# First projection cut into quarters of x and of its weights, with idle products ahead of them and the parameter rows moved ahead of the second megabyte of weights

## The chip, the cores and the metric

One core of a Trainium2 chip runs the whole program. The metric is device time in microseconds (us). The engines are TensorE (PE; its weight loads are shown apart as PEld), VectorE (DVE), ScalarE (ACT), GpSimd (POOL) and SyncE (SP). In this kernel SP issues nearly all DMAs. Each engine works through its own instructions in a fixed order, and an instruction that waits holds up everything behind it on its engine.

## The reference, cut to what matters

One decoder layer on x of 256 tokens by 1024 channels, float32:

```python
def mixer(x, w_in, ...):
    proj = jnp.einsum("bsd,de->bse", x, w_in)          # 1024 -> 10264 columns
    (a_in, gdn_qkv, gdn_beta_in, gdn_decay_in, gdn_gate_in,
     sb_qkv, gla_qkv, gla_lr, gla_gate_in, merge_in) = jnp.split(proj, offsets, axis=-1)
    ...
    qkv = jax.nn.silu(causal_depthwise_conv(gdn_qkv, gdn_conv_w))
    g = -jnp.exp(gdn_a_log) * jax.nn.softplus(gdn_decay_in + gdn_dt_bias)
    ...                                                # four mixers, gates, output projection
x = layer_norm(DN_ALPHA * x + mixer(x, ...), ln1_g, ln1_b)
x = layer_norm(DN_ALPHA * x + moe(x, ...), ln2_g, ln2_b)   # 16 experts, top 2
```

The change concerns the first 256 of those 10264 columns (the first part of `gdn_qkv`) and the loads ahead of the second 256.

## The kernel before

The kernel streams `w_in` in pieces of 256 columns, 1 MB each. A piece goes through three raw buffers (`fetch`, line 109). `parts` (line 119) splits each half of it into a high part `whi` (ACT, rounded to the type fp32r) and the remainder `wlo` (DVE). x is split the same way into `xh` and `xl`. `proj_cm` (line 282) then makes, for each half of 128 columns, 16 products with `whi` (lines 271 and 275) and 8 with `wlo` (line 280), 48 a piece, each of 256 columns on PE.

The steps of the mixers stand in a list written by hand, `ORDER` (line 40); it begins `bi.0 cc bi.1 bi.2 cq.0 bi.3 sm`. `bi.0`, `bi.1`, `bi.2` are the first three pieces (here w0, w1, w2), `cc` makes small constants (`aexp` among them, line 353, out of the row `gdn_a_log`). A scheduler puts the instructions of PE, ACT, DVE and POOL into an order of its own by what it thinks will be ready; SP keeps the order of the program.

At the start SP issues x in four pieces of 256 KB (line 145), w0 in two halves of 128 columns, w1 in one piece (line 146), then eleven rows of parameters into the tile `prm_r` (line 165) and two rows, `gdn_a_log` and `gdn_dt_bias`, into `hp8` (lines 177 and 178), then w2 and the rest. A SP DMA uses one of eight completion counters in turn, and its issue waits until the DMA eight places ahead of it has landed. PE transposes x in four groups (line 263), and ACT and DVE split them. `taps` (line 335) transposes `prm_r` on PE (`pp`) and makes the convolution weights `cwh` out of it, which the evictions of w0's products need.

Of the kernel before, what the change touches and what calls it, by code (L numbers as in the profile page):

```python
# [8 lines left out]
F32 = mybir.dt.float32  # L9
# [9 lines left out]
S = 256  # L19
# [32 lines left out]
def trunk(ctx: ExitStack, tc: tile.TileContext, a, out):  # L52
# [55 lines left out]

    def fetch(src, cuts=1):
        k, n = src.shape[1], src.shape[2]  # L110
        turn_raw()
        raw = rwp[rwo[-1]].tile([128, 2048], F32, name="raw", tag="raw")[:, :k * n]
        raw = raw.rearrange("p (k c) -> p k c", k=k)
        for c in range(cuts):
            cs = slice(c * n // cuts, (c + 1) * n // cuts)
            Q.dma_start(raw[:, :, cs], src[:, :, cs])
        return raw

    def parts(raw, k0, nk, c0, n, one=None):

# [4 lines left out]
        src = raw[:, k0:k0 + nk, c0:c0 + n]  # L125
        cuts = (slice(0, nk),) if one is None else (slice(0, nk // 2), slice(nk // 2, nk))
        for c in cuts:
            if one is None:
                A.copy(hi, src)  # L129
            else:  # L130
                A.activation(hi[:, c], src[:, c], AF.Copy, scale=one)  # L131
        for c in cuts:
            V.tensor_tensor(lo[:, c], src[:, c], hi[:, c].bitcast(F32), op=OP.subtract)  # L133
        return hi, lo
# [54 lines left out]
    def late_loads():  # L189
# [67 lines left out]
    xl = xtp.tile([128, 8, S], F32R, name="xl")  # L257
    one0 = cst.tile([128, 1], F32, name="one0")
    for kg in range(2):
        for n in range(2):  # L260
            p = pb("pxt")
            for k in range(4):
                T.transpose(p[:, k, :], x0[n][:, (4 * kg + k) * 128:(4 * kg + k + 1) * 128], ident)
            split(p, xh[:, 4 * kg:4 * kg + 4, n * 128:(n + 1) * 128],
                  xl[:, 4 * kg:4 * kg + 4, n * 128:(n + 1) * 128])
    A.activation(one0, xh[:, 4, 0:1].bitcast(F32), AF.Copy, scale=0.0, bias=1.0)

# [126 lines left out]
    def b_in(ci):  # L394
# [1034 lines left out]
```

## Time and profile before

| | us |
|---|---|
| median of 3 runs | 622.49 (621.53 to 623.31) |
| the profiled execution's own time | 622.35 |
| its span in the trace | 620.6 |
| PE busy | 585.3 (94%) |
| DVE busy | 322.3 (52%) |
| ACT busy | 252.2 (41%) |

The profiled execution stands at the median, and 1.75 us of it lie outside its span. The page's strip of 40 slices of 15.5 us shows where PE is not full: the first slice, a stretch in the middle, and the last ones. Its column of the granted clock reads full in the first slices; there the spacing of the products tells the clock: 256 columns in 0.213 us are 1.2 columns a ns, in 0.118 us near 2.2, so the first belongs to the level of 1.2 GHz and the second to that of 2.4 GHz.

### The profile page before, as it was taken

What the parts mean: (1) busy time and instruction counts of PE and PEld (TensorE: products, weight loads), DVE (VectorE), ACT (ScalarE), POOL (GpSimd) and SP (SyncE); (2) the same over time, 40 slices, a digit from 0 to 9 for tenths busy, and PEclk for the clock granted to TensorE, in tenths of its full rate; (3) what the DMA queues carried; (4) which work ended last, traced back from release to release, by engine and by line L of the source; (5) the groups of instructions that cost most, each with busy time, mean ns of one, the idle gap of its engine ahead of it and who ended that gap; (6) DMA issues with size and microseconds to landing.
All of it is one profiled execution on the core that took longest, in us unless ns stands there. A gap on an engine that the chain in (4) does not pass through costs nothing.

```text
span 620.6 us, 10538 instructions
## 1 busy us (share of the span) xinstructions
PE 585.3 (94%) x4225; PEld 458.0 (74%) x4225; DVE 322.3 (52%) x639; ACT 252.2 (41%) x413; POOL 23.1 (4%) x57
## 2 busy tenths in 40 slices
PE   6999999999988999999999999999999999999970
PEld 5999999999888999999999999533543634533340
DVE  3798888687566976565566655551210210300154
ACT  5557654473569784444444445210211211210121
POOL 3000010000111000000000000000000000000002
PEclk9999999999999999999999998999999999999995
DMA  7877454632221446588999795899999999999912
GB/s 206 240 227 179 137 181 122 215 110 70 69 70 50 155 127 203 197 295 299 376 336 336 272 404 183 295 330 410 419 412 409 417 413 409 418 415 408 418 70 72
DMA packets 86658, 160.93 MB, mean 259 GB/s; under 512 B 9990, under 2 KB 56444, under 8 KB 86604
## 3 DMA queue, kind: packets, MB, share of 16 engines
q1 hardware_dynamic: 86476, 159.94, 71.4%
q8 instruction: 35, 0.57, 0.4%
q0 software_dynamic: 128, 0.26, 0.2%
q14 instruction: 19, 0.16, 0.1%
HBM read 159.01 MB, written 1.18 MB: 258 GB/s over the span
## 4 chain that ended last, share of the span: by engine, by line
PE 70%; issue 12%; DVE 6%; DMA 6%; ACT 3%; POOL 1%; SPq 1%; POOLq 0%; DVEq 0%; ACTq 0%
PE wg L1277 9%; PE pd L1288 9%; PE wu L1277 8%; PE pcm L271 7%; PE pcm L280 7%; PE pcm L275 7%; DMA raw<-in_w_in_dram 3%; PE pxg L1198 3%; PE pbr L271 2%; PE pbr L280 2%; PE pbr L275 2%; DMA ew<-in_w_down_dram 2%; DVE wlo L133 1%; PE pwo L271 1%; PE py L1297 1%
## 5 line engine op out<-in xcount | busy, mean ns | idle before, releaser
L133 DVE TENSOR_TENSOR wlo<-raw,whi 128x1024 fp32r<-128x1024 f32 (+1 forms) x106 | 126.0, 1201 | 53.6 <-ACT whi L129 53.0
L129 ACT CAST whi<-raw 128x1024 fp32r<-128x1024 f32 x102 | 105.9, 1048 | 101.3 <-PE pcm L275 41.7
L271 PE MATMUL pcm<-xh,whi 128*128 128x256 f32 x512 | 126.0, 284 | 2.4 <-ACT whi L131 1.5
L275 PE MATMUL pcm<-xl,whi 128*128 128x256 f32 x512 | 125.0, 282 | 0.0
L271 PEld LDWEIGHTS pcm<-xh,whi 128*128 128x128 f32 x512 | 97.2, 190 | 3.3 <-ACT whi L131 1.9
L275 PEld LDWEIGHTS pcm<-xl,whi 128*128 128x128 f32 x512 | 97.3, 190 | 0.1
L280 PE MATMUL pcm<-xh,wlo 128*128 128x256 f32 x512 | 72.2, 282 | 0.2
L280 PEld LDWEIGHTS pcm<-xh,wlo 128*128 128x128 f32 x512 | 65.5, 189 | 0.7 <-DVE wlo L133 0.6
L101 DVE TENSOR_TENSOR dd<-pd,dd 128x512 fp32r<-128x512 f32 (+1 forms) x18 | 11.4, 631 | 95.2 <-ACT dd L100 95.2
L1288 PE MATMUL pd<-ew,sh 128*64 128x512 f32 (+1 forms) x288 | 57.7, 546 | 2.1 <-DMA ew<-in_w_down_dram 1.3
L1277 PE MATMUL wu<-ew,xg 128*64 128x512 f32 x256 | 57.4, 593 | 0.0
L1277 PE MATMUL wg<-ew,xg 128*64 128x512 f32 x256 | 56.7, 595 | 0.6 <-issue 0.6
L1288 PEld LDWEIGHTS pd<-ew,sh 128*64 128x64 f32 x288 | 20.5, 137 | 37.2 <-issue 29.4
L1277 PEld LDWEIGHTS wu<-ew,xg 128*64 128x64 f32 x256 | 18.5, 137 | 36.2 <-issue 34.4
L1277 PEld LDWEIGHTS wg<-ew,xg 128*64 128x64 f32 x256 | 18.1, 137 | 33.5 <-issue 31.8
L271 PE MATMUL ptm<-whi,xh 128*128 128x256 f32 x128 | 32.6, 287 | 0.0
L271 PE MATMUL pbr<-yth,whi 128*128 128x256 f32 x128 | 32.1, 284 | 0.0
L275 PE MATMUL pbr<-ytl,whi 128*128 128x256 f32 x128 | 32.1, 282 | 0.0
L273 PE MATMUL ptm<-whi,xl 128*128 128x256 f32 x128 | 31.6, 281 | 0.0
L100 ACT CAST dd<-pd 128x512 fp32r<-128x512 f32 (+1 forms) x18 | 9.7, 539 | 48.5 <-PE pd L1288 48.5
L1205 ACT ACTIVATE xg<-pxg,gbp 128x128 f32<-128x128 f32 x32 | 13.3, 456 | 36.8 <-DVE xg L1204 35.8
L1318 DVE SCALAR_TENSOR_TENSOR sh<-wu,cw,sh 128x512 f32<-128x512 f32 x8 | 6.0, 750 | 40.2 <-PE wu L1277 40.1
(410 smaller groups left out, 884.9 us busy)
## 6 DMA issues: line engine op xcount, KB each, us to landing
raw<-in_w_in_dram SPq DMA_DIRECT2D x39, 1024.0 KB, 5.3
ew<-in_w_gate_dram SPq DMA_DIRECT2D x64, 512.0 KB, 10.0
ew<-in_w_up_dram SPq DMA_DIRECT2D x64, 512.0 KB, 9.9
ew<-in_w_down_dram SPq DMA_DIRECT2D x64, 512.0 KB, 9.9
raw<-in_w_branch_dram SPq DMA_DIRECT2D x8, 1024.0 KB
raw<-in_w_out_dram SPq DMA_DIRECT2D x4, 1024.0 KB
x<-in_x_dram SPq DMA_DIRECT2D x4, 256.0 KB, 5.1
raw<-in_w_in_dram SPq DMA_DIRECT2D x2, 512.0 KB
```

What stands on the lines that cost most here:

```text
L100: A.copy(hi, ps)
L101: V.tensor_tensor(lo, ps, hi.bitcast(F32), op=OP.subtract)
L129: A.copy(hi, src)
L133: V.tensor_tensor(lo[:, c], src[:, c], hi[:, c].bitcast(F32), op=OP.subtract)
L271: T.matmul(o, sh(k), mh(k), start=first and k == 0, stop=False)
L273: T.matmul(o, sl(k), mh(k), start=False, stop=False)
L275: T.matmul(o, sh(k), ml(k), start=False, stop=False)
L280: T.matmul(o, sl(k), mh(k), start=False, stop=last and k == kt - 1)
L1198: P(T.matmul(ps[kg][:, k, :], x[:, n, 128 * (2 * kg + k):128 * (2 * kg + k) + 128], oh[n], start=first and n == 0, stop=last and n == 1))
L1205: A.activation(xg[1][:, 2 * kg + k, :], ps[kg][:, k, 128:256], AF.Identity, scale=g_, bias=b_)
L1277: P(T.matmul(p[r, :], xg[pr][:, k, r], W[pr, (nm, e, k // 2)][:, k % 2, :], start=k == 0, stop=k == 7))
L1288: P(T.matmul(p[r, :], hT[:, k, r], W[pr, ("wd", e, k)][:, 0, c0:c1], start=k == 0, stop=k == 3))
```

## The change

- x is loaded in eight pieces of 128 KB and w0 in four of 256 KB (256 rows of the weights each), a quarter of x and a quarter of w0 in turn.
- The thirteen rows of parameters (`prm_r`, `hp8`) follow w0; w1 comes behind them, and w2 is fetched with it.
- `first_proj` replaces `proj_cm` for w0: 14 idle products of a tile of zeros on PE, the transposes of the first quarter of x, 8 more idle products, and then, quarter by quarter, the split of the weights, 8 products with the high part, the transposes of the next quarter of x, and 4 products with the low part. They are kept in this order among themselves; other instructions may be placed between them.
- The helpers for a split in halves (`cuts`, `one`) and the constant `one0` go.

```diff
-    for h in range(2):
-        for n in range(2):
-            Q.dma_start(x0[n][:, 512 * h:512 * h + 512], xin[:, n, 512 * h:512 * h + 512])
-    raw0 = [fetch(w_in[:, :, C_GQ + 256 * j:C_GQ + 256 * j + 256], 2 - j) for j in range(2)]
+    w0 = w_in[:, :, C_GQ:C_GQ + 256]
+    raw0 = [fetch(w0, 0)]
+    for q in range(4):
+        cs = slice(256 * q, 256 * q + 256)
+        for n in range(2):
+            Q.dma_start(x0[n][:, cs], xin[:, n, cs])
+        Q.dma_start(raw0[0][:, 2 * q:2 * q + 2], w0[:, 2 * q:2 * q + 2])
...
+    raw0 += [fetch(w_in[:, :, C_GQ + 256 * j:C_GQ + 256 * j + 256]) for j in (1, 2)]
...
+    def warm(n):
+        for _ in range(n):
+            K(T.matmul(idle, wz[:, 0:128], wz, start=True, stop=True))
+    def x_part(q):
+        ps = pb("pxt", (128, 2, S))
+        for n in range(2):
+            for k in range(2):
+                K(T.transpose(ps[:, k, n * 128:(n + 1) * 128], x0[n][:, (2 * q + k) * 128:(2 * q + k + 1) * 128], ident))
+        split(ps, xh[:, 2 * q:2 * q + 2, :], xl[:, 2 * q:2 * q + 2, :], keep=K)
+    def first_proj():
+        p = pmm.tile([128, 2, S], F32, name="pcm", tag="mm")
...
+        warm(14)
+        x_part(0)
+        warm(8)
+        for q in range(4):
...
+            K(A.copy(hi, raw))
+            K(V.tensor_tensor(lo, raw, hi.bitcast(F32), op=OP.subtract))
+            for k in range(2 * q, 2 * q + 2):
+                for b in range(2):
+                    for x in (xh, xl):
+                        K(T.matmul(p[:, b, :], hi[:, k % 2, 128 * b:128 * b + 128], x[:, k, :],
+                                   start=q == 0 and k == 0 and b == 0 and x is xh, stop=False))
+            if q < 3:
+                x_part(q + 1)
+            low(q)
+        return p
...
-        p = proj_cm(C_GQ + 256 * ci, raw0[ci] if ci < 2 else None, one0 if ci == 0 else None)
+        p = first_proj() if ci == 0 else proj_cm(C_GQ + 256 * ci, raw0[ci] if ci < 3 else None)
```

On SP, before: `raw_109` is w0 in two halves and `raw_112` is w1, ahead of the first parameter rows.

```order
L116 DMA raw_109<-in_w_in_dram 128x8x128 x2
L116 DMA raw_112<-in_w_in_dram 128x8x256
L165 DMA prm_r_114<-in_gdn_conv_w_dram 48x128
L165 DMA prm_r_114<-in_gdn_norm_w_dram 1x128
L165 DMA prm_r_114<-in_gla_b_gate_dram 4x128
```

On SP, now: the end of the parameter rows; `raw_143` is w1, `raw_145` w2 and `raw_496` the piece of `cq.0`.

```order
L163 DMA prm_r_118<-in_rg_b_x_dram 4x128
L163 DMA prm_r_118<-in_rg_lambda_dram 4x128
L163 DMA prm_r_118<-in_ln1_g_dram 8x128
L163 DMA prm_r_118<-in_ln1_b_dram 8x128
L175 DMA hp8_132<-in_gdn_a_log_dram 128x4
L176 DMA hp8_132<-in_gdn_dt_bias_dram 128x4
L117 DMA raw_143<-in_w_in_dram 128x8x256
L117 DMA raw_145<-in_w_in_dram 128x8x256
```

All thirteen rows now stand ahead of w1. The row `in_rg_b_x` is the eighth DMA behind the last quarter of w0 (before, it was the eighth behind w1), so its issue waits for the landing of that quarter.

On ACT, before: the four groups of x, the four quarters of the high part of w0, both halves of w1 (`whi_328`, `whi_356`), and then `aexp`, which reads the row `hp8`.

```order
L131 ACTIVATE whi_217<-raw_109,one0_176 128x512 x2
L131 ACTIVATE whi_247<-raw_109,one0_176 128x512 x2
L129 CAST whi_328<-raw_112 128x1024
L129 CAST whi_356<-raw_112 128x1024
L353 ACTIVATE aexp_209<-hp8_128 128x4
L406 ACTIVATE gq_215<-pcm_216,cwh_206 128x256
```

On ACT, now: `pxt_212`, `pxt_239`, `pxt_260` and `pxt_283` are the four quarters of x, `raw_105` is w0 and `raw_143` is w1.

```order
L102 CAST xh_182<-pxt_239 128x512
L295 CAST whi_227<-raw_105 128x512
L392 ACTIVATE aexp_190<-hp8_132 128x4
L102 CAST xh_182<-pxt_260 128x512
L295 CAST whi_271<-raw_105 128x512
L102 CAST xh_182<-pxt_283 128x512
```

`aexp` moved from behind the splits of w0 and w1 to a place between the second and the third quarter of x. The splits of the third and fourth quarter stand behind it.

On PE, before: the last products of w0 (`pcm_216`), the transpose `pp` of the parameter rows, and the first products of w1 (`pcm_327`).

```order
L275 MATMUL pcm_216<-xl_175,whi_247 128x256
L280 MATMUL pcm_216<-xh_174,wlo_248 128x256 x8
L337 MATMUL pp_277<-ident_98,prm_r_114 128x128
L271 MATMUL pcm_327<-xh_174,whi_328 128x256
L275 MATMUL pcm_327<-xl_175,whi_328 128x256
```

On PE, now: `whi_271` and `wlo_272` are the parts of the third and fourth quarter of w0.

```order
L300 MATMUL pcm_197<-xl_183,whi_271 128x256
L272 MATMUL pxt_283<-ident_98,x0_103 128x128 x2
L272 MATMUL pxt_283<-ident_98,x0_104 128x128 x2
L283 MATMUL pcm_197<-xh_182,wlo_272 128x256 x4
L376 MATMUL pp_308<-ident_98,prm_r_118 128x128
L300 MATMUL pcm_197<-xh_182,whi_271 128x256
```

`pp` moved ahead of the products of the last quarter, so these stand behind the landing of all eleven rows in `prm_r`. Behind the step `sm` every engine's order is that of before.

## Rows read from the trace of the kernel before

**Rows 1.** The page's strip of the span in 40 slices of 15.5 us: busy tenths of PE and of the DMA engines.

```profile
PE   6999999999988999999999999999999999999970
...
DMA  7877454632221446588999795899999999999912
```

**Rows 2.** The table of windows; each row gives the stretch, its length, then busy us (and count) of PE, PEld, DVE, ACT, POOL, the granted clock, the DMA share and GB/s.

```profile
0.00:10.00 10.00, 4.17 (x16) 3.00 (x16) 2.89 (x7) 4.38 (x8) 5.08 (x29) 1.00 0.84 239
10.00:15.00 5.00, 4.88 (x23) 4.88 (x24) 2.79 (x5) 3.28 (x6) 0.00 (x0) 1.00 0.50 159
...
20.00:60.00 40.00, 39.70 (x335) 39.24 (x335) 36.15 (x96) 24.63 (x37) 0.00 (x0) 1.00 0.81 231
...
450.00:584.00 134.00, 134.00 (x664) 56.52 (x662) 20.27 (x41) 20.91 (x41) 0.00 (x0) 1.00 1.03 413
```

**Rows 3.** The chain of work that ended last, followed back from 20 us: start us, us, what. L165 are the parameter rows, L177 and L178 the two rows of `hp8`, L116 pieces of `w_in`.

```profile
3.98 9.74 DMA raw<-in_w_in_dram
...
13.74 0.25 SPq L165
...
15.05 0.36 SPq L177
...
15.46 0.43 SPq L178
...
15.93 0.43 SPq L116
```

**Rows 4.** The waits of SP's queue in the first 20 us: us in total, times, longest us.

```profile
SPq L165 <- DMA raw<-in_w_in_dram: 2.9, 2, 2.6
```

**Rows 5.** The timeline of ACT: start us, us, line, operation, count, and in brackets the idle time before it with its releaser.

```profile
4.75 0.59 ACT L100 CAST xh<-pxt 128x512 fp32r<-128x512 f32 x1 [2.67 <-PE pxt L263]
...
10.88 1.34 ACT L131 ACTIVATE whi<-raw,one 128x512 fp32r<-128x512 f32 x2 [0.20 <-DMA raw<-in_w_in_dram]
13.75 2.00 ACT L129 CAST whi<-raw 128x1024 fp32r<-128x1024 f32 x2 [1.53 <-DMA raw<-in_w_in_dram]
17.59 0.20 ACT L353 ACTIVATE aexp<-hp 128x4 f32<-128x4 f32 x1 [1.85 <-DMA hp<-in_gdn_a_log_dram]
...
21.51 1.05 ACT L129 CAST whi<-raw 128x1024 fp32r<-128x1024 f32 x1 [1.83 <-DMA raw<-in_w_in_dram]
```

**Rows 6.** The timeline of PE in the first projection and at the start of the second (17.98), same columns.

```profile
6.62 1.97 PE L263 MATMUL pxt<-ident,x 128*128 128x128 f32 x8 [0.32 <-DMA x<-in_x_dram]
10.12 0.58 PE L271 MATMUL pcm<-xh,whi 128*128 128x256 f32 x1 [1.53 <-ACT whi L131]
10.51 0.41 PE L275 MATMUL pcm<-xl,whi 128*128 128x256 f32 x1
...
13.71 1.58 PE L280 MATMUL pcm<-xh,wlo 128*128 128x256 f32 x8
15.12 0.28 PE L271 MATMUL pcm<-xh,whi 128*128 128x256 f32 x1
...
17.00 1.11 PE L280 MATMUL pcm<-xh,wlo 128*128 128x256 f32 x8
17.95 0.27 PE L337 MATMUL pp<-ident,prm_r 128*128 128x128 f32 x1
17.98 0.36 PE L271 MATMUL pcm<-xh,whi 128*128 128x256 f32 x1
```

**Rows 7.** The timeline of DVE, same columns: the low parts of w1, and the eviction of the parameter rows.

```profile
14.83 2.36 DVE L133 TENSOR_TENSOR wlo<-raw,whi 128x1024 fp32r<-128x1024 f32 x2 [1.88 <-ACT whi L129]
...
18.26 0.29 DVE L338 COPY prm<-pp 128x128 f32<-128x128 f32 x1 [0.26 <-PE pp L337]
```

**Rows 8.** The table of windows again, by 1 us (columns as in group 2; the last two are the DMA share and GB/s).

```profile
1.00:2.00 1.00, 0.00 (x0) 0.00 (x0) 0.00 (x0) 1.00 (x1) 0.95 (x4) 1.00 0.25 29
...
10.00:11.00 1.00, 0.88 (x4) 0.88 (x5) 0.90 (x2) 0.81 (x3) 0.00 (x0) 1.00 1.08 345
...
12.00:13.00 1.00, 1.00 (x6) 1.00 (x6) 0.94 (x2) 0.22 (x1) 0.00 (x0) 1.00 0.36 107
13.00:14.00 1.00, 1.00 (x7) 1.00 (x6) 0.00 (x0) 0.25 (x1) 0.00 (x0) 1.00 0.02 7
...
18.00:19.00 1.00, 1.00 (x10) 1.00 (x9) 0.70 (x5) 0.13 (x1) 0.00 (x0) 1.00 1.01 352
```

**Rows 9.** The same by 1 us around a gap of PE late in the program; the third column from the right is the granted clock.

```profile
380.00:381.00 1.00, 0.87 (x9) 0.77 (x7) 0.45 (x2) 0.58 (x1) 0.00 (x0) 1.00 0.55 193
381.00:382.00 1.00, 0.51 (x3) 0.28 (x3) 0.78 (x4) 0.50 (x2) 0.00 (x0) 1.00 1.00 410
382.00:383.00 1.00, 0.68 (x5) 0.58 (x6) 0.40 (x5) 0.98 (x2) 0.00 (x0) 1.00 1.09 426
...
384.00:385.00 1.00, 1.00 (x7) 1.00 (x6) 0.99 (x8) 1.00 (x2) 0.00 (x0) 0.50 1.03 418
```

**Rows 10.** The chain of work that ended last, near the end: start us, us, what.

```profile
581.01 3.26 PE wu L1277 x15
584.27 10.28 DMA ew<-in_w_down_dram
...
594.59 2.37 PE pd L1288 x18
```

**Rows 11.** The waits of PE from 20 to 60 us: us in total, times, longest us.

```profile
PE pcm L271 <- DVE splq L326: 0.3, 1, 0.3
```

More of the change, by code (lines that the diff above doesn't have):

```diff
@@ L96, in pb, with split @@
         return pbr.tile(list(shape), F32, name=name, tag="pb")
-    def split(ps, hi, lo, scale=None):
+    K = tc.keep_in_program_order
+    def split(ps, hi, lo, scale=None, keep=lambda i: i):
         if scale is None:
-            A.copy(hi, ps)
-            V.tensor_tensor(lo, ps, hi.bitcast(F32), op=OP.subtract)
+            keep(A.copy(hi, ps))
+            keep(V.tensor_tensor(lo, ps, hi.bitcast(F32), op=OP.subtract))
         else:
@@ L107, in trunk, with fetch @@
     w_in = a["w_in"][0].rearrange("(k p) c -> p k c", p=128)
-    def fetch(src, cuts=1):
+    def fetch(src, rows=None):
         k, n = src.shape[1], src.shape[2]
@@ L113, in fetch, with parts @@
         raw = raw.rearrange("p (k c) -> p k c", k=k)
-        for c in range(cuts):
-            cs = slice(c * n // cuts, (c + 1) * n // cuts)
-            Q.dma_start(raw[:, :, cs], src[:, :, cs])
+        if rows is None:
+            Q.dma_start(raw, src)
         return raw
-    def parts(raw, k0, nk, c0, n, one=None):
+    def parts(raw, k0, nk, c0, n):
         hi = wst.tile([128, 1024], F32R, name="whi", tag="whi", bufs=NHI)[:, :nk * n]
@@ L125, in parts @@
         src = raw[:, k0:k0 + nk, c0:c0 + n]
[L126 to L133, printed above, removed]
+        A.copy(hi, src)
+        V.tensor_tensor(lo, src, hi.bitcast(F32), op=OP.subtract)
         return hi, lo
@@ L257, in trunk @@
     xl = xtp.tile([128, 8, S], F32R, name="xl")
-    one0 = cst.tile([128, 1], F32, name="one0")
-    for kg in range(2):
-        for n in range(2):
[L261 to L266, printed above, removed]
+    wz = cst.tile([128, S], BF16, name="wz")
@@ new lines, in trunk, with low @@
+    V.memset(wz, 0.0)
+    idle = pb("idle", (128, S))
+    def warm(n):
[3 more added lines that the diff above has]
+        ps = pb("pxt", (128, 2, S))
+        for n in range(2):
+            for k in range(2):
[3 more added lines that the diff above has]
+        p = pmm.tile([128, 2, S], F32, name="pcm", tag="mm")
+        hl = {}
+        def low(q):
+            for k in range(2 * q, 2 * q + 2):
+                for b in range(2):
+                    K(T.matmul(p[:, b, :], hl[q // 2][1][:, k % 4, 128 * b:128 * b + 128], xh[:, k, :],
+                               start=False, stop=k == 7 and b == 1))
+        warm(14)
+        x_part(0)
+        warm(8)
+        for q in range(4):
+            if q % 2 == 0:
+                hl[q // 2] = [wst.tile([128, 1024], F32R, name=nm, tag=nm, bufs=NHI).rearrange("p (k c) -> p k c", k=4)
+                              for nm in ("whi", "wlo")]
+            raw = raw0[0][:, 2 * q:2 * q + 2]
+            hi, lo = (t[:, 2 * (q % 2):2 * (q % 2) + 2] for t in hl[q // 2])
+            K(A.copy(hi, raw))
+            K(V.tensor_tensor(lo, raw, hi.bitcast(F32), op=OP.subtract))
+            for k in range(2 * q, 2 * q + 2):
+                for b in range(2):
+                    for x in (xh, xl):
[5 more added lines that the diff above has]
+        return p
@@ L280, in mm3, with proj_cm @@
                 T.matmul(o, sl(k), mh(k), start=False, stop=last and k == kt - 1)
-    def proj_cm(c0, raw=None, one=None):
+    def proj_cm(c0, raw=None):
         if raw is None:
@@ L287, in proj_cm @@
         for b in range(2):
-            hi, lo = parts(raw, 0, 8, 128 * b, 128, one)
+            hi, lo = parts(raw, 0, 8, 128 * b, 128)
             mm3(p[:, b, :], lambda k: hi[:, k, :], lambda k: lo[:, k, :],
```

## The prediction

> **What bounds the kernel now.** I read first the strip and the table of windows. PE is busy 4.17 of the first 10 us, 4.88 of the next 5, 39.70 of the 40 behind them and 134.00 of 134 in the long last stage [rows 1, 2]. So PE is the bound nearly everywhere, and what the change can win lies ahead of about 18 us. What happens to PE there is passed on one for one: the later steps hang on each other, the weight stream of the last stage is issued as PE gives buffers back, and the end itself runs from a PE step at 581.01 through a DMA of 10.28 us back to PE [rows 10]. The orders of all engines behind the step `sm` are the same. I therefore price the change by one number, the time at which PE begins w1's products, 17.98 now [rows 6].
>
> Then the first 18 us. PE waits for x and w0 until 10.12. Its products begin at half clock: 15 of them take 13.71 − 10.51 = 3.20 us, 0.213 each; from about 14.8 they take (17.00 − 15.12)/16 = 0.118, the full clock [rows 6]. The whole first projection is 48 products, 5.7 us at full clock, and it fills 10.12 to 17.95. w1 lands at 13.72, and only then does the row `b_x` go out (13.74): SP waited 2.6 us for that landing. Six issues later, at 15.93, goes w2 [rows 3, 4]. The DMA engines are nearly idle meanwhile: 7 GB/s in the microsecond from 13, 352 again in that from 18 [rows 8]. ACT waits 1.85 us for the row `gdn_a_log`, but has split w1 by then, so nobody waits for it [rows 5].
>
> **What the change removes.** x and w0 are used as they land, so most of the first projection, 7.8 us from 10.12, could run beside the loads. The best it can do is set by the last quarter: its landing, 0.67 us for the high part (1.34 for two halves [rows 5]), 12 products of 0.118, some 2.1 us. When that landing comes, T, is not in the trace. From above: the same two megabytes had landed by 10.88, when ACT could start the second half of w0 [rows 5]. From below: 2.1 MB at 345 GB/s [rows 8] are 6.1 us; transfers begin shortly before 2 (29 GB/s in the microsecond from 1), and the last megabyte landed 1.3 us behind the end of its traffic, which stops at about 12.4 (share 0.36 in that microsecond [rows 8]) and is done at 13.72 [rows 3]; that makes 9.4. Nothing lets it come earlier, since the bytes are the same. I take T = 10.2, the middle. By this alone PE would be free for w1 at 12.3 instead of 17.98. Three moves take it back.
>
> **SP.** `b_x` now waits for T, not for w1. Behind it stand three rows, `gdn_a_log`, `gdn_dt_bias`, and then w1. By the rows of now `gdn_a_log` goes out 15.05 − 13.74 = 1.31 us behind `b_x` and the next megabyte 15.93 − 13.74 = 2.19 [rows 3]. So w1 is issued at T + 2.19 = 12.4. A megabyte issued onto idle queues is there after 5.6 us (w2: 15.93 to 21.51, when ACT starts on it [rows 3, 5]), so w1 lands at 18.0 instead of 13.72. Its split (1.05) puts the first product at 19.05 at best. That alone is 1.1 late.
>
> **ACT.** `aexp` stands now ahead of the splits of the third and fourth quarter and needs `gdn_a_log`. From `b_x` to `aexp` it is 17.59 − 13.74 = 3.85 us now [rows 3, 5], so ACT stands until T + 3.85 = 14.05 with x and w0 long landed. Queued behind it are the high parts of both last quarters, and PE and DVE wait for these. Then `aexp` 0.20, the split of the third quarter of x 0.59 [rows 5], of the weights 0.67: PE restarts at 15.5.
>
> The Trainium skill ("DMA: Bandwidth & Descriptors", "Anatomy of one DMA — SWDGE (gpsimd) path") gives a DMA a fixed cost of about 2.0 us, and its "Rules for kernel authors" call transfers under 64 KB mostly overhead, a rule against putting thirteen of them ahead of a megabyte. The row here took 17.59 − 15.05 = 2.54 us; with the page's figure the sum would be 0.5 less, 625.2 where it is 625.7. The measured row decides.
>
> **PE.** The first two quarters need x and w0's first half. x as a whole is in by 6.62 now, when PE's last eight transposes stop waiting [rows 6], which is about as many bytes. With two splits (1.3) and at most 16 slow slots (3.4) they are done by 11.5. From there to 15.5 PE stands for 4 us. The 22 idle products (22 × 0.213 = 4.7 us at most, of which the first 14 run while PE waited for x anyway) so raise a clock that is lost again: at 381 to 383 PE was busy 0.51 and 0.68 of a microsecond, and the clock of 384 to 385 is 0.50 [rows 9]. The Trainium skill ("TensorE: Matmul & The Clock Gate", "The HAM clock gate") says the same, that an array left idle falls back to 1.2 GHz; these rows agree, and without this fall the sum would be the second rival below.
>
> Restart at 15.5: 8 products of 0.213 (17.2), 4 transposes (0.9, 18.1); ACT then splits the fourth quarter, 0.59 + 0.67 and about 0.05 of handing over: 19.4. Beside that run 4 low products and `pp`, whose rows are in by then (the last one is issued at T + 1.0, two and a half more to land, 13.7). Last come 12 products. Now the clock took 4.6 us of running to rise (10.12 to about 14.8 [rows 6]); the same from 15.5 is 20.1. So 3 at 0.213 and 9 at 0.118 end at 21.2. w1's split ran on ACT from 19.4 to 20.5, hidden. **w1's products begin at 21.2, 3.2 later than 17.98.** If the clock is back by 19.4 it is 20.8, if only behind the last product 22.0.
>
> **What follows.** DVE splits w1 later too: 2.36 us that stood at 14.83, when it was free, now stand behind the eviction `prm` [rows 7]. DVE has 36.15 busy of 40 [rows 2], and PE once waited 0.3 for it [rows 11]. With PE 3.2 later DVE gets that time as well, so I charge nothing; if that cover were short, up to 1 us. The first split of x loses one instruction (`one0`), DVE gains one memset: nothing, both while waiting for x.
>
> The sum goes on the profiled execution: 622.35 + 3.2 = 625.55; the median is 0.14 above that execution, so 625.7.
>
> **Rivals.**
> 1. ACT is released early and w1's landing is the gate. For it: ACT's stop needs only one small row, and w1's landing is gate enough by itself. Against: both hang on the same T, and ACT's part is measured. Then PE ends w0 early, idles until 19.05 and restarts at half clock; 4.6 us at that clock cost about 2.0 over full: 3.1 later, 625.6.
> 2. The clock stays at 2.4 GHz through the 4 us (the idle products having raised it). For it: the gaps in the middle of the program are passed over. Against: rows 9. Then 15.5, 0.94 for 8 products, 0.45 for transposes, 1.31 for the split, 1.42 for 12: 19.65, 1.7 later, 624.2.
> 3. Not slower: SP's rows do not wait for landings. Twelve issues of some 0.46 end at 6.3; eleven rows of 0.33 put `gdn_a_log` at 10.0, landed at 12.5, so PE restarts at 14.0 after a shorter gap and, at full clock, ends w0 at 18.1; w1 issued at 10.8 is in by 16.4. That is 0.15 later, 622.6, no change. It decides from the point where `b_x` leaves before T. Against it: the 2.6 us that `b_x` waits now [rows 4].
>
> **How the numbers follow.** Forecast 0.62; rival 1 0.14; rival 2 0.10; rival 3 0.10; 0.04 for a gain whose place I do not see (part of the 5.7 us kept after all). A difference under 0.3% (1.9 us, so 620.6 to 624.4) is about what a measurement here cannot tell from no change. Faster: 0.04. Same: rival 3 and most of rival 2, 0.16. Slower: 0.80. T's bounds move the forecast by −0.8 and +0.7, the clock by −0.4 and +0.8, DVE's cover by up to +1, so 624.5 to 627.6 for rivals 0 and 1; the range goes down to 623.0 to take in rival 2, and leaves out rival 3, the gain and a small tail above.
>
> **What the changed profile would show.** On ACT, `aexp` at about 14 with an idle stretch of some 4 us ahead of it released by the DMA of `hp`, and the third split of x behind it. On SP, `b_x` at about 10.2 and w1 at 12.4. On PE, nothing from about 11.5 to 15.5, products spaced 0.213 there after, and w1's first product at 21 instead of 18. From there every step later by the same amount. I am wrong if `aexp` is done by 11, if w1's first product stands at 18 or earlier, or if a later stage gives the 3 us back.

## The result and the profile after

The changed kernel takes 628.75 us (median of 5, 626.94 to 630.72) against 622.49 for the kernel before beside it: 1.0103 times as long, 95% interval 1.0082 to 1.0124. It is slower, as forecast, but by 6.3 us and not by 3.2, and outside the range of 623.0 to 627.6. The profiled execution is the median one; its span is 626.9 us, 6.3 more than before.

The start came out nearly as worked out. On SP (timeline: start us, us, line, operation; a row can hold several issues), `b_x` goes out at 10.69, so T was 10.7 where 10.2 was taken; `gdn_a_log` follows at 12.01 and w1 at 12.89, where it went out at 3.98 before [rows 3]:

```profile
10.69 0.25 SPq L163 DMA_DIRECT2D prm_r<-in_rg_b_x_dram  x1
...
12.01 0.36 SPq L175 DMA_DIRECT2D hp<-in_gdn_a_log_dram  x1
...
12.89 11.01 SPq L117 DMA_DIRECT2D raw<-in_w_in_dram  x4
```

On ACT (timeline, in brackets the idle time ahead and its releaser), `aexp` stands 5.23 us for the row of `gdn_a_log`, with the third quarter's splits behind it:

```profile
14.54 0.21 ACT L392 ACTIVATE aexp<-hp 128x4 f32<-128x4 f32 x1 [5.23 <-DMA hp<-in_gdn_a_log_dram]
14.65 0.57 ACT L102 CAST xh<-pxt 128x512 fp32r<-128x512 f32 x1
15.11 0.62 ACT L295 CAST whi<-raw 128x512 fp32r<-128x512 f32 x1
18.75 0.59 ACT L102 CAST xh<-pxt 128x512 fp32r<-128x512 f32 x1 [3.02 <-PE pxt L272]
19.23 0.62 ACT L295 CAST whi<-raw 128x512 fp32r<-128x512 f32 x1
```

On PE, the products of the second quarter still ran at 0.12 us each (10.14 to 10.26), the full clock. The third quarter waits 4.21 us for ACT and starts at 0.21 us a product (16.17 to 16.38), the fourth follows at 19.91, and w1's first product stands at 21.52, against 17.98 [rows 6] and the 21.2 of the forecast:

```profile
10.14 0.28 PE L300 MATMUL pcm<-xl,whi 128*128 128x256 f32 x1
10.26 0.28 PE L300 MATMUL pcm<-xh,whi 128*128 128x256 f32 x1
...
15.79 0.58 PE L300 MATMUL pcm<-xh,whi 128*128 128x256 f32 x1 [4.21 <-ACT whi L295]
16.17 0.41 PE L300 MATMUL pcm<-xl,whi 128*128 128x256 f32 x1
16.38 0.41 PE L300 MATMUL pcm<-xh,whi 128*128 128x256 f32 x1
...
19.91 0.39 PE L300 MATMUL pcm<-xh,whi 128*128 128x256 f32 x1 [0.53 <-ACT whi L295]
...
21.52 0.28 PE L310 MATMUL pcm<-xh,whi 128*128 128x256 f32 x1
```

The table of windows (columns as in [rows 2]) shows the granted clock at 0.50 behind that gap, which is the level of 1.2 GHz, rising again from 18 to 19, then PE full to 60, and the last stage:

```profile
16.00:17.00 1.00, 1.00 (x5) 1.00 (x6) 0.54 (x1) 0.00 (x0) 0.00 (x0) 0.50 1.06 372
18.00:19.00 1.00, 1.00 (x8) 1.00 (x6) 0.00 (x0) 0.25 (x1) 0.00 (x0) 0.62 1.09 352
20.00:60.00 40.00, 39.96 (x337) 39.65 (x338) 37.12 (x99) 25.90 (x41) 0.00 (x0) 1.00 0.76 207
450.00:584.00 134.00, 134.00 (x662) 56.45 (x660) 18.89 (x39) 20.37 (x41) 0.00 (x0) 1.00 1.03 409
```

The last row is the one that was not forecast. In the same stretch the kernel before moved 413 GB/s [rows 2], this one 409, both with the DMA engines' share at 1.03. At the end PE's `pd` (the products of the experts' last weights) waits for `w_down` three times, and its last run begins at 599.98, not at 594.59 [rows 10]:

```profile
597.47 0.65 PE L1327 MATMUL pd<-ew,sh 128*64 128x256 f32 x2 [0.62 <-DMA ew<-in_w_down_dram]
598.72 0.65 PE L1327 MATMUL pd<-ew,sh 128*64 128x256 f32 x2 [0.60 <-DMA ew<-in_w_down_dram]
599.98 2.37 PE L1327 MATMUL pd<-ew,sh 128*64 128x256 f32 x18 [0.62 <-DMA ew<-in_w_down_dram]
```

Places that stand in both kernels in the same order, read from the timelines, show where the 6.3 us arise. `pwt` and `prg` belong to the mixers; `wg`, `wu` and `pd` are the products with the experts' three weights:

| start of | before | after | later by |
|---|---|---|---|
| w1's first product | 17.98 | 21.52 | 3.54 |
| `psmall`, first product of `sm` | 41.16 | 44.13 | 2.97 |
| `pwt`, first transpose | 185.15 | 189.00 | 3.85 |
| `prg`, first product | 211.58 | 216.89 | 5.31 |
| `wg`, first product of the last stage | 394.01 | 397.69 | 3.68 |
| `wu`, last product | 587.28 | 591.16 | 3.88 |
| `pd`, last product | 601.68 | 607.07 | 5.39 |
| the span's end | 620.6 | 626.9 | 6.3 |

So some 3 us come at the start, 1.5 between the last `wu` and the last `pd`, 0.9 behind it. The steps between (+0.9 up to `pwt`, +1.5 near 212, −1.6 ahead of 394) stand in runs without the change too, or fall out either way (below).

### The profile page after: what moved, and what is told of

It is laid out like the page before. It is cut to its first block, busy times and chain, and to the rows that moved or that the text cites. A ratio compares the mean times of both kernels' runs of the same rounds, so it can differ in the third digit from the quotient of the medians.

```text
span 626.9 us, 10585 instructions
## 1 busy us (share of the span) xinstructions
PE 587.6 (94%) x4247; PEld 458.2 (73%) x4247; DVE 321.6 (51%) x640; ACT 251.7 (40%) x412; POOL 23.0 (4%) x57
## 4 chain that ended last, share of the span: by engine, by line
PE 70%; issue 12%; DVE 6%; DMA 6%; ACT 3%; POOL 1%; SPq 0%; POOLq 0%; DVEq 0%; ACTq 0%
PE wg L1316 9%; PE wu L1316 9%; PE pd L1327 9%; PE pcm L310 7%; PE pcm L319 7%; PE pcm L314 7%; PE pxg L1237 2%; DMA raw<-in_w_in_dram 2%; PE pbr L310 2%; PE pbr L319 2%; PE pbr L314 2%; DMA ew<-in_w_down_dram 2%; DVE wlo L128 1%; PE pwo L310 1%; PE py L1336 1%
## 5 line engine op out<-in xcount | busy, mean ns | idle before, releaser
L128 DVE TENSOR_TENSOR wlo<-raw,whi 128x1024 fp32r<-128x1024 f32 x102 | 123.4, 1220 | 50.1 <-ACT whi L127 49.9
L310 PE MATMUL pcm<-xh,whi 128*128 128x256 f32 x496 | 120.3, 281 | 0.6 <-ACT whi L127 0.6
L314 PE MATMUL pcm<-xl,whi 128*128 128x256 f32 x496 | 119.6, 280 | 0.0
L310 PEld LDWEIGHTS pcm<-xh,whi 128*128 128x128 f32 x496 | 93.1, 188 | 0.9 <-ACT whi L127 0.8
L314 PEld LDWEIGHTS pcm<-xl,whi 128*128 128x128 f32 x496 | 93.1, 188 | 0.1
L319 PE MATMUL pcm<-xh,wlo 128*128 128x256 f32 x496 | 69.4, 280 | 0.8 <-DVE wlo L128 0.7
L319 PEld LDWEIGHTS pcm<-xh,wlo 128*128 128x128 f32 x496 | 62.9, 188 | 1.3 <-DVE wlo L128 1.2
L1316 PEld LDWEIGHTS wu<-ew,xg 128*64 128x64 f32 x256 | 18.9, 137 | 35.9 <-issue 33.3
## 6 DMA issues: line engine op xcount, KB each, us to landing
ew<-in_w_up_dram SPq DMA_DIRECT2D x64, 512.0 KB, 10.2
ew<-in_w_down_dram SPq DMA_DIRECT2D x64, 512.0 KB, 10.2
```

The costliest lines, as they stand in the source:

```text
L128: V.tensor_tensor(lo, src, hi.bitcast(F32), op=OP.subtract)
L310: T.matmul(o, sh(k), mh(k), start=first and k == 0, stop=False)
L314: T.matmul(o, sh(k), ml(k), start=False, stop=False)
L319: T.matmul(o, sl(k), mh(k), start=False, stop=last and k == kt - 1)
L1316: P(T.matmul(p[r, :], xg[pr][:, k, r], W[pr, (nm, e, k // 2)][:, k % 2, :], start=k == 0, stop=k == 7))
```

## The experiments

Medians of each kernel and of the kernel before on the same chip; `sm`, `wu` and `pd` are the starts named above, in the profiled execution; GB/s over 450 to 584 us. The profiled execution can lie off its kernel's median (before_64 by +2.2 us, aexp_late by −1.8), and w1's first product moves between executions: the four kernels before with a padded `one0` have the order of before and show it at 16.9 to 18.7, with `sm` at 41.2 to 41.6.

| kernel | us | before | ratio, 95% | w1's first | `sm` | last `wu` | last `pd` | GB/s |
|---|---|---|---|---|---|---|---|---|
| before (profile) | | | | 18.0 | 41.2 | 587.3 | 601.7 | 413 |
| after | 628.75 | 622.49 | 1.0103, 1.0082–1.0124 | 21.5 | 44.1 | 591.2 | 607.1 | 409 |
| aexp_late | 628.28 | 622.02 | 1.0108, 1.0082–1.0135 | 19.7 | 43.9 | 590.0 | 604.7 | 409 |
| no_idle | 628.02 | 622.02 | 1.0095, 1.0072–1.0118 | 21.1 | 43.7 | 591.8 | 607.7 | 409 |
| x8w4 | 622.79 | 622.02 | 1.0007, 0.9990–1.0024 | 16.8 | 41.4 | 589.1 | 602.9 | 413 |
| early12 | 630.64 | 622.02 | 1.0142, 1.0117–1.0166 | 16.2 | 47.0 | 593.8 | 609.7 | 409 |
| before_480 | 624.35 | 621.85 | 1.0039, 1.0021–1.0056 | 18.7 | 41.6 | 588.5 | 604.3 | 409 |
| after_wz240 | 628.78 | 621.85 | 1.0110, 1.0087–1.0133 | 20.9 | 43.5 | 591.6 | 607.2 | 409 |
| best | 622.13 | 621.85 | 0.9995, 0.9975–1.0014 | 15.5 | 37.3 | 585.3 | 601.1 | 409 |
| best_chain | 623.55 | 621.85 | 1.0037, 1.0018–1.0057 | 16.9 | 39.7 | 586.9 | 601.5 | 409 |
| no_idle_addr | 624.39 | 621.72 | 1.0039, 1.0023–1.0055 | 21.4 | 44.0 | 591.8 | 604.6 | 413 |
| best_addr | 620.32 | 621.72 | 0.9977, 0.9962–0.9992 | 16.6 | 39.4 | 585.3 | 599.4 | 413 |
| best_wz144 | 620.20 | 621.72 | 0.9972, 0.9957–0.9987 | 16.1 | 38.8 | 584.9 | 597.4 | 413 |
| before_256 | 622.70 | 621.72 | 1.0010, 0.9996–1.0024 | 17.7 | 41.4 | 587.2 | 601.2 | 413 |
| before_128 | 623.50 | 621.97 | 1.0030, 1.0015–1.0046 | 18.0 | 41.6 | 587.4 | 603.1 | 409 |
| before_64 | 623.64 | 621.97 | 1.0031, 1.0014–1.0049 | 16.9 | 41.2 | 589.1 | 605.0 | 409 |
| act_gate | 630.45 | 621.97 | 1.0127, 1.0098–1.0155 | 23.3 | 46.1 | 594.7 | 609.7 | 409 |

### The start: two waits and a chain

**aexp_late.** `K(...)` ties an instruction into the written order of its engine.

```diff
-        A.activation(aexp, hp8[:, 0:4], AF.Exp)
+        K(A.activation(aexp, hp8[:, 0:4], AF.Exp))
```

> The changed kernel, with aexp alone tied behind the splits of w0 on ACT; SP's order is untouched, so w1 is still issued near 12.9 us. Theory (two gates in a row, ACT's wait for gdn_a_log and w1's landing): the 4.21 us that PE stands ahead of the third quarter shrink to about 1, w0's last products end near 16 instead of 21.5, but w1 lands near 18.2 and its first product stands at about 19.3. PE has then stood some 3 us and starts w1 at 0.213 us a product, which gives back about 2 us: w2's products begin within 0.5 us of where they begin now, and the time stays at 628.0 to 629. Rival (ACT's wait is the whole cause): w1's first product near 16 to 17, time 623 to 625. Rival (the start hardly matters, the 2.7 us that 628.75 is beyond the shift of 3.5 at the start are a matter of the later stages): time within 0.5 us of 628.75 too, but with the late loss differently large although the order behind sm is the same.

The first theory held. ACT no longer stands, yet w1 lands only at 18.58, PE waits 2.49 us for its split, and the time is that of the changed kernel within the intervals. ACT's rows show a third thing: the quarters come 2.93 us apart, and each waits for PE's transposes, not for a DMA:

```profile
8.39 0.59 ACT L102 CAST xh<-pxt 128x512 fp32r<-128x512 f32 x1 [2.02 <-PE pxt L272]
...
11.32 0.59 ACT L102 CAST xh<-pxt 128x512 fp32r<-128x512 f32 x1 [1.83 <-PE pxt L272]
...
14.26 0.59 ACT L102 CAST xh<-pxt 128x512 fp32r<-128x512 f32 x1 [1.83 <-PE pxt L272]
...
18.58 2.00 ACT L127 CAST whi<-raw 128x1024 fp32r<-128x1024 f32 x2 [3.21 <-DMA raw<-in_w_in_dram]
```

```profile
16.55 0.63 PE L283 MATMUL pcm<-xh,wlo 128*128 128x256 f32 x4
19.67 0.39 PE L310 MATMUL pcm<-xh,whi 128*128 128x256 f32 x1 [2.49 <-ACT whi L127]
```

**act_gate** takes away the other wait: w1 ahead of the rows, eleven of these on GpSimd's queue, `aexp` where the changed kernel has it.

```diff
+    raw0 += [fetch(w_in[:, :, C_GQ + 256 * j:C_GQ + 256 * j + 256]) for j in (1,)]
     rows = {}
...
-        Q.dma_start(prm_r[nrow:nrow + n, :], ap)
+        G.dma_start(prm_r[nrow:nrow + n, :], ap)
...
+            if q == 1:
+                K(A.activation(aexp, hp8[:, 0:4], AF.Exp))
```

> The changed kernel with the eleven rows of prm_r on GpSimd's queue and w1 on SP straight behind w0, ahead of the two rows of hp8; aexp is tied to its place on ACT between the second and the third quarter, the transpose of the rows ahead of w1's products. So w1 lands early, near 14, and ACT's wait for gdn_a_log stays, since this row comes behind w1 now. Theory (the two waits stand beside each other, and either gives the same late start): gdn_a_log lands near 14, PE stands 4 us ahead of the third quarter as in the changed kernel, w1's first product at 21 to 21.8, 628 to 629.5. Rival (w1's landing was the gate that cost the time): w1's first product at 18 or earlier and 624 to 626.

The mechanism is the theory's, its size was short: the row behind w1 lands at 15.7, not 14, w1's first product stands at 23.3, not 21 to 21.8, and the time is 630.45, not 628 to 629.5.

```profile
15.72 0.21 ACT L305 ACTIVATE aexp<-hp 128x4 f32<-128x4 f32 x1 [5.86 <-DMA hp<-in_gdn_a_log_dram]
```

```profile
16.96 0.58 PE L302 MATMUL pcm<-xh,whi 128*128 128x256 f32 x1 [4.84 <-ACT whi L297]
```

So either wait alone gives the late start, and taking one away wins nothing. With both away (best_chain, below, which also issues w2 early and ties more of the order) it is 5.2 us less than the changed kernel at the same addresses (after_wz240, below).

**no_idle** drops `warm(14)` and `warm(8)`.

> The changed kernel without its 22 idle products; all else is untouched. Theory (the clock that they raise is lost again in the 4.21 us in which PE stands): the first two quarters run at 0.213 us a product instead of 0.118 and end near 12 instead of 11.5, the third quarter starts at 15.8 as it does now, w1's first product stands at 21.5 within 0.2, and the time is that of the changed kernel within 1 us (627.7 to 629.7). Rival (the idle products are worth what the lower clock costs, 16 products and 8 transposes of the first quarters): w1's first product 2 us later or more, 630.5 or more. Rival (the idle products themselves cost time): 0.5 to 1 us faster.

As in theory, though the first two quarters take until 13.9, not 12: PE reaches its gap at 13.9 instead of 11.6 and leaves it at 15.53 (15.79 with the idle products), so the clock they raised had been lost.

```profile
11.06 0.58 PE L298 MATMUL pcm<-xh,whi 128*128 128x256 f32 x1 [0.34 <-ACT whi L293]
...
15.53 0.38 PE L298 MATMUL pcm<-xh,whi 128*128 128x256 f32 x1 [1.67 <-ACT whi L293]
```

**early12** issues w1 and w2 ahead of the rows and ties w1's splits and products, then the rows' transpose, then `aexp`, behind w0.

```diff
+            p = first_proj()
+            v.p1 = proj_cm(C_GQ + 256, raw0[1], K)
             taps()
```

> The changed kernel with w1 and w2 issued ahead of the parameter rows, w1's products directly behind w0's on PE, and the transpose of the rows, the evictions and aexp behind these. Theory (the order of SP and ACT took back what the quarters won): w0's products end near 14, w1 lands near 13.7 and its first product stands at about 14.8, w2 lands near 16.7 and its first product stands near 20.6, against 23.7 in the kernel before; carried one for one that is 619.4 (618.5 to 620.5). Rival (w0's eviction, now behind about 21, or the rows become the gate of the third piece): w2's first product at 23 to 24, 622 to 623. Rival (a later stage gives an early start back): w2 early, but the time still 622 or more.

The gain missed, and so did the numbers of the rivals; the first rival had named the right thing, the late evictions, but not their size. w1's first product came at 16.2 and w2's at 21.9, but the scheduler put DVE's copy of the rows (`prm`) behind the low part of the fourth piece, which ACT split only from 24.9; w0 and w1 could not be evicted, and PE stood 5.87 us:

```profile
26.00 1.23 DVE L128 TENSOR_TENSOR wlo<-raw,whi 128x1024 fp32r<-128x1024 f32 x1 [5.36 <-ACT whi L127]
27.14 0.28 DVE L377 COPY prm<-pp 128x128 f32<-128x128 f32 x1
```

```profile
33.66 0.55 PE L310 MATMUL pcm<-xh,whi 128*128 128x256 f32 x1 [5.87 <-DVE splq L364]
```

**best** mends this (its tile of zeros has 240 columns, as in after_wz240 below): the rows go out on GpSimd's queue from the start, their transpose stands ahead of w1's products, and the next quarter's transposes stand ahead of this quarter's products.

```diff
+            if q < 3:
+                x_part(q + 1)
             for k in range(2 * q, 2 * q + 2):
...
-            if q < 3:
-                x_part(q + 1)
             low(q)
```

> The changed kernel with the tile of zeros of 240 columns; w1 and w2 issued straight behind w0 on SP; the thirteen parameter rows on GpSimd's queue from the start; the transposes and split of the next quarter of x ahead of the products of this one; then on PE the transpose of the rows, w1's products; aexp behind these. Theory (three things took back the gain of the quarters: the rows ahead of w1, ACT's chain from quarter to quarter, the addresses): w0 ends near 13, w1 lands near 13.7 and its first product stands at 15, w2's first at 21 against 23.6 in the kernel before, and the time is 619 to 620.5. Rival (the rows on GpSimd's queue land late and hold PE ahead of w1): w1's first product at 17 or later and 621 to 623. Rival (an early start is given back later): w2's first product at 21 and still 622.

The start held: w0 is done at 13.75, and w1, landed at 14.38, begins at 15.47, 2.5 us earlier than before; `sm` is 3.8 earlier. GpSimd's thirteen issues take some half a us each, and nobody waits for the rows. The time did not follow: 622.13, no change (0.9975 to 1.0014).

```profile
13.75 0.27 PE L376 MATMUL pp<-ident,prm_r 128*128 128x128 f32 x1
15.47 0.38 PE L310 MATMUL pcm<-xh,whi 128*128 128x256 f32 x1 [1.45 <-ACT whi L127]
```

```profile
9.09 0.59 ACT L102 CAST xh<-pxt 128x512 fp32r<-128x512 f32 x1 [1.03 <-PE pxt L272]
...
10.90 0.59 ACT L102 CAST xh<-pxt 128x512 fp32r<-128x512 f32 x1 [0.70 <-PE pxt L272]
...
14.38 2.00 ACT L127 CAST whi<-raw 128x1024 fp32r<-128x1024 f32 x2 [2.36 <-DMA raw<-in_w_in_dram]
```

```profile
1.54 0.74 POOL L164 DMA_DIRECT2D prm_r<-in_gdn_conv_w_dram  x1
...
7.86 0.55 POOL L177 DMA_DIRECT2D hp<-in_gdn_dt_bias_dram  x1
```

**best_chain** is best with the transposes behind the products again.

> The kernel best, but with the transposes of the next quarter of x behind the products of this one, as in the changed kernel. Theory (the quarters are a chain of their own: PE's transposes, ACT's two splits, PE's products, 2.93 us each in the run with aexp held back, slower than the quarters land): the fourth quarter is split at about 14.3 and w0 ends near 16.5 instead of 13, w1's first product at 16.5 and w2's at 22: 620.5 to 621.5, one to 1.5 us more than best. Rival (the landings set the pace and the chain is hidden): the same as best within 0.5 us.

The theory of the chain held: quarters 2.93 apart, w1 at 16.9, 1.4 us slower than best. The time, 623.55, is above the 620.5 to 621.5 that it gave, since best was slower than expected too.

```profile
11.15 0.59 ACT L102 CAST xh<-pxt 128x512 fp32r<-128x512 f32 x1 [1.83 <-PE pxt L272]
...
14.08 0.58 ACT L102 CAST xh<-pxt 128x512 fp32r<-128x512 f32 x1 [1.83 <-PE pxt L272]
```

### The end: addresses of the weight buffers

In every run so far with the tile of zeros `wz` (512 bytes a partition, 480 in best and best_chain, where `one0` took 32) the last stage moved 409 GB/s. `wz` stands ahead of most tiles on its side of SBUF, which so begin 480 or 448 bytes higher. As the built programs place them, the stream of the last stage goes round 38 buffers `ew`. Ten of these begin at multiples of 256 bytes before and none after; the other 28 lie on the other side of SBUF, at 224 bytes past a multiple, and do not move. The expectations below count 20 buffers, of which 14 move and six stay. Four of these 14 are each loaded once, ahead of the last stage, and six are too few for those that stay.

**x8w4**: the kernel before with x in eight DMAs and w0 in four, for the number of DMAs alone.

> The kernel before, with x loaded in eight DMAs and w0 in four, in the old order and all used as before. It has the six DMAs more of the changed kernel, so the eight completion counters stand at the same turn in all later stages, and nothing else of it. Theory (the losses of the changed kernel behind the start belong to its start or to the execution, not to the number of DMAs): 622.5 within 1 us, the weights of the last stage at 412 to 418 GB/s as before. Rival (the turn of the counters slows the later streams): 624 to 626, with the last stage at 408 to 410 GB/s and the last down products waiting as in the changed kernel.

```profile
450.00:584.00 134.00, 134.00 (x664) 56.48 (x662) 19.97 (x41) 20.91 (x41) 0.00 (x0) 1.00 1.03 413
```

No change within the interval, at 413 GB/s: the rate is not a matter of the number of DMAs. One thing is: from the last `pd` to the span's end it is 19.7 us (622.6 − 602.9), as in the changed kernel (19.8), where the kernel before takes 18.9 and the four with a padded `one0` below 18.6 to 18.9. All kernels with the six DMAs more take 19.4 to 20.1. That is the 0.9 us of the table.

**before_480** changes no instruction, only a size:

```diff
-    one0 = cst.tile([128, 1], F32, name="one0")
+    one0 = cst.tile([128, 128], F32, name="one0")[:, 0:1]
```

> The kernel before with the constant one0 made 512 bytes a partition instead of 32 (only its first column is used): every later tile on that side of SBUF lies 480 bytes higher, at the addresses of the changed kernel, and no instruction or order differs. In the kernel before 14 of the 20 weight buffers of the last stage begin at a multiple of 64 bytes, in the changed kernel and here none of these do (they begin 32 bytes past one). Theory (the 408 to 410 GB/s of the last stage in every kernel that has the tile of zeros, against 409 to 418 in those that have not, come from these addresses): the last stage at 408 to 410 GB/s here too, the down products at the end waiting, and 624 to 626. Rival (the rate belongs to the later start or to the changed order of the loads): 412 to 418 GB/s and 622 within 1 us.

```profile
450.00:584.00 134.00, 134.00 (x662) 56.45 (x660) 20.27 (x41) 20.88 (x41) 0.00 (x0) 1.00 1.03 409
```

2.5 us slower (1.3 to 3.5 by the ratio's interval), and the rate falls to 409: the addresses alone do it.

**after_wz240** (`S - 16` columns in `wz` and `idle`, a shift of 448 bytes):

> The changed kernel with the tile of zeros 240 columns wide instead of 256 (480 bytes), so that the later tiles lie 448 bytes higher than in the kernel before, at multiples of 64 bytes where they were so there. The 22 idle products are 240 columns long; nothing else differs. Theory (addresses): the last stage at 412 to 418 GB/s, and of the 6 to 7 us that the changed kernel loses 2 to 3 come back: 625 to 627; what stays is the start, some 3 us. Rival (the loss is all the start's): 628 to 629 and 408 to 410 GB/s.

```profile
450.00:584.00 134.00, 134.00 (x664) 56.51 (x662) 18.90 (x39) 20.34 (x40) 0.00 (x0) 1.00 1.03 409
```

This theory fell: multiples of 64 bytes do not bring the rate back. The addresses differ in multiples of 256, which the next three test on the kernel before, with `one0` of 72, 40 and 24 columns:

> The kernel before with one0 made 288 bytes a partition: later tiles 256 bytes higher, no instruction or order different. Theory (multiples of 256 bytes): 409 to 418 GB/s in the last stage and 622 within 1 us, no loss. Rival (any move of these buffers against the six that stay costs the rate): 408 to 410 GB/s, 624 to 625, as with 480 bytes.

```profile
450.00:584.00 134.00, 134.00 (x662) 56.45 (x660) 20.27 (x41) 20.91 (x41) 0.00 (x0) 1.00 1.03 413
```

> The kernel before with one0 made 160 bytes a partition: later tiles 128 bytes higher, the ten weight buffers that begin at a multiple of 256 bytes then begin 128 past one (still a multiple of 128). Theory (multiples of 256 bytes): the last stage at 408 to 410 GB/s in every slice, 624 to 625. Rival (multiples of 128, or of 64, suffice): 409 to 418 GB/s and 622 within 1 us.

```profile
450.00:584.00 134.00, 134.00 (x663) 56.46 (x661) 20.26 (x41) 20.89 (x41) 0.00 (x0) 1.00 1.03 409
```

> The kernel before with one0 made 96 bytes a partition: later tiles 64 bytes higher. Of the 20 weight buffers four, other ones than before, then begin at a multiple of 256 bytes instead of ten. Theory (the share of buffers at multiples of 256 bytes sets the mean rate): between the two rates, 410 to 412 GB/s over 450 to 550 us where the kernel before has 413 and the moved ones 409, and 623 to 624. Rival (all that counts is whether the buffers lie at multiples of 64 bytes): 413 GB/s and 622 within 1 us. Rival (only the ten): 409 and 624 to 625.

256 bytes keep the rate, 128 and 64 lose it, and with it 1.9 us in both by the ratios (before_128 came out somewhat under what was expected). before_64 moves 409, not the 410 to 412 expected, but it does not test the share of buffers: the four that reach multiples of 256 there are those loaded once, ahead of the stage.

The traces show when the rate is lost. Counted back from the last transfer, the ten buffers come up in the kernel before between about 529 and 546 us, and only others between 503 and 528. Rows of before, before and before_480:

```profile
503.00:528.00 25.00, 25.00 (x120) 9.60 (x118) 2.90 (x5) 3.25 (x6) 0.00 (x0) 1.00 1.03 409
530.00:552.00 22.00, 22.00 (x124) 11.40 (x122) 4.10 (x11) 4.42 (x10) 0.00 (x0) 1.00 1.03 418
530.00:552.00 22.00, 22.00 (x122) 11.38 (x120) 4.86 (x13) 4.62 (x11) 0.00 (x0) 1.00 1.03 409
```

So 413 is a mean: 418 GB/s while the ten come up and for a few transfers behind them, 409 while the 28 others do. What the move takes away is the faster stretches; the others lose nothing.

**no_idle_addr** is no_idle without `wz`, a 32-byte constant in its place, so at the addresses of before.

> The changed kernel without its idle products and without their tile of zeros; a constant of 32 bytes stands in the place of one0, so that every later tile has the address that it has in the kernel before. Theory (addresses make some 2.4 us of the loss, the start the rest): the last stage goes back to slices of 409 to 418 GB/s, w1's first product stays near 21, and the time is 2 to 3 us under that of the changed kernel without idle products, at 625 to 626.5, some 3 to 4 over the kernel before. Rival (the addresses cost only the kernel before something, since a later start hides them): 627.5 to 629.

```profile
450.00:584.00 134.00, 134.00 (x662) 56.44 (x660) 18.88 (x39) 20.33 (x40) 0.00 (x0) 1.00 1.03 413
```

The pair no_idle and no_idle_addr shows the same in the changed kernel: the last `wu` stands at 591.8 in both, the last `pd` at 607.7 and 604.6. The medians are 3.6 us apart, a little more than expected; the two were timed on different chips, and by their ratios to the kernel before it is 3.5 us, which the intervals leave open from 1.7 to 5.2. What is left of the change, 1.0039 or 2.4 us (1.4 to 3.4), is the start together with what the six DMAs cost behind the last `pd`.

**best_addr** and **best_wz144** give best the old addresses, the one without idle products, the other with `wz` and the idle products 144 columns wide (a shift of 256).

> The kernel best without idle products and their tile, at the addresses of the kernel before. Theory (best gained 3.9 us at the start and gave 2.4 back by the addresses of the last stage; the idle products are worth nothing where w1's landing, near 14, decides when its products begin): w1's first product within 0.7 us of best's 15.47, the last stage at 409 to 418 GB/s, 619 to 620.5. Rival (the idle products carry the gain, since without them all of w0 runs at 0.213 us a product): w1's first product at 17 or later, 621 to 622.5.

```profile
16.61 0.36 PE L302 MATMUL pcm<-xh,whi 128*128 128x256 f32 x1
```

> The kernel best with the tile of zeros, and so the idle products, 144 columns wide: later tiles lie 256 bytes higher than in the kernel before, and the ten weight buffers that begin at a multiple of 256 bytes there do so here. Theory (multiples of 256 bytes are what the faster slices of the last stage need): 409 to 418 GB/s and 619 to 620.5. Rival (something else of the addresses, as the distance to the six buffers that do not move): 408 to 410 GB/s and 621.5 to 622.5.

```profile
450.00:584.00 134.00, 134.00 (x663) 56.45 (x661) 20.27 (x41) 20.85 (x41) 0.00 (x0) 1.00 1.03 413
```

Both are faster than both kernels, 0.9977 and 0.9972, by 1.4 and 1.5 us in the medians against the kernel before. The idle products are not quite worth nothing here, against what was expected. Without them w0's products last until w1's begin at 16.6; with them w0 is done at 13.75 (best) and 14.06 (best_wz144), but w1's landing lets its products begin only at 15.5 and 16.1. The time does not show the difference.

## Why the prediction was wrong, and where it was right

- **SP and ACT: right.** T + 2.19 gave 12.4 for w1's issue (12.89), T + 3.85 gave 14.05 for `aexp` (14.54). The half us is T itself.
- **PE: right in the sum.** Restart 15.5 (15.79), the half clock behind the gap, w1's first product 21.2 (21.52). Inside it two misses nearly cancel: the clock was back between 18 and 19 and not at 20.1, and the fourth quarter began 4.1 us behind the restart and not 3.9. Rivals 2 and 3 fell with these rows. The idle products were lost, as said (no_idle).
- **"By this alone PE would be free for w1 at 12.3": wrong in its reason.** The landings of the quarters do not set the pace; transposes, two splits and eight products do, 2.93 us a quarter (aexp_late, best_chain). Without ACT's stop w0's last four products begin at 16.55 and w1 at 19.67. With the transposes moved ahead w0 is over at 13.75 (best).
- **Rival 1** put its price within 0.1 us of the forecast's, and aexp_late shows that this was so: two gates, one price.
- **"I therefore price the change by one number": the step that failed.** An unchanged order behind `sm` was taken for an unchanged program. The list of parts charged the new constant one memset, "nothing"; its 480 bytes moved the weight buffers, and the stream of the last stage fell from 413 to 409 GB/s. That alone measured 1.9 to 2.5 us in kernels that differ in nothing else (before_64, before_128, before_480). An estimate from the rates: from 400 us on, 148 transfers of 512 KB are 77.6 MB, 187.9 us at 413 GB/s and 189.7 at 409, so 1.8. The six DMAs more were not priced either; they cost 0.8 to 0.9 behind the last `pd`.
- **How far this adds up.** Start and six DMAs 2.4 (no_idle_addr), addresses 1.9 to 2.5: 4.3 to 4.9 of the 6.3 measured, whose interval reaches down to 5.1. With the 3.5 of the two no_idle runs it would be 5.9. Whether the addresses cost more in the changed kernel than in the kernel before is not shown.
- **The range.** The prediction's own bounds add up to 625.7 + 0.7 + 0.8 + 1 = 628.2 at the top, not 627.6; the measured 628.75 lies above that too.
- **Why that reaches the end.** [rows 10] were read as a DMA of 10.28 us that hangs on a PE step. [rows 2] show the DMA engines' share at 1.03 beside PE at 134.00 of 134. At 413 GB/s 512 KB take 1.27 us, so a DMA of 10.28 us stands behind some seven others (an estimate): it waits in a full queue, and the stream's rate sets when the last `w_down` lands. That PE is full there did not make it the only bound. The Trainium skill ("DMA: Bandwidth & Descriptors", "Specifications") gives about 358 GB/s as the limit of HBM for one core, which is half of a stack's 716, and 435 for the fabric. The runs' 409 and 413, with one core at work, lie above the first and below the second; the measured rate decides.
- **DVE's cover, charged nothing: right to 60 us**, where DVE is busy 37.12 of 40 and PE 39.96. From `sm` to `pwt` another 0.9 of the "up to 1" came in this execution and 0.2 in no_idle_addr; that DVE is the cause is not shown.
- **"From there every step later by the same amount": roughly.** 3.54 at w1 is 2.97 at `sm`, and in aexp_late 1.7 is 2.8. By the medians the start with the six DMAs is 2.4 us (1.4 to 3.4) against the 3.2 forecast, within the bounds given.

What stays open: why multiples of 256 bytes matter, and whether the 28 other buffers would gain from them too; and what in the 0.8 to 0.9 us behind the last `pd` hangs on the six DMAs. Two steps of the first table go with the execution, not with the change. Near 205 us a piece of `w_in` lands late in some:

```profile
208.74 1.05 ACT L127 CAST whi<-raw 128x1024 fp32r<-128x1024 f32 x1 [2.33 <-DMA raw<-in_w_in_dram]
```

x8w4, whose `sm` starts as before, has the same step (`prg` 1.8 later), before_256 has not. And the gap of PE near 387 left the clock at full level here, where it fell to 0.50 in [rows 9]. Of the seventeen profiles, after, aexp_late and best_wz144 keep it, and need 180.7 to 180.8 us from `prg` to `wg`; the other fourteen, the kernel before among them, lose it and need 182.4 to 182.6:

```profile
386.00:387.00 1.00, 0.63 (x4) 0.29 (x3) 1.00 (x5) 0.18 (x1) 0.00 (x0) 1.00 0.96 393
387.00:388.00 1.00, 0.62 (x4) 0.52 (x4) 0.20 (x2) 0.98 (x3) 0.00 (x0) 1.00 1.06 434
388.00:389.00 1.00, 0.81 (x7) 0.81 (x8) 0.68 (x6) 0.99 (x4) 0.00 (x0) 1.00 0.57 229
```

## What to carry to other kernels

That its memset costs nothing does not make a new constant free: look where the later tiles come to lie, above all the targets of a stream that keeps the DMA engines full; a run with a padded tile in the old kernel prices it alone. Where two waits end at nearly the same time, each has the whole price and removing one gains nothing, so take both away before judging either. And work cut into pieces that land one by one is only as fast as the chain from piece to piece: let what depends on the next piece's landing stand ahead of what can wait.

## What the hardware showed that was not expected

- The address of an SBUF buffer changes a DMA stream's rate: 413 GB/s with ten of 38 buffers at multiples of 256 bytes (moves of 0 and 256), 409 with moves of 64, 128, 448 and 480; 418 while the ten come up, 409 while the others do.
- Small rows cost GpSimd some half a us a DMA to issue, thirteen from 1.54 to 8.41 in best, and were used at 13.75 without a wait; on SP in the changed kernel they hold w1's issue back to 12.89. No run changes this alone.
- A gap of PE at the same place lowered the granted clock to 0.50 in fourteen profiles and left it at 1.00 in three; between the kernel before and the changed one this is 1.6 us.
